# Combined FFN weights summed by accumulating DMAs, three units begun early, and six k-tiles held back, in a two-layer decoder trunk

## The chip, the cores and the metric

One core of a Trainium2 chip runs the whole program. The time is device microseconds of one execution. Three timed runs of the kernel before gave 1096.71, 1097.17 and 1097.77 us, median 1097.17.

Engines: PE multiplies matrices (the stationary operand is loaded by PEld, which overlaps), DVE is the vector engine, ACT the scalar engine, POOL the third elementwise engine, and SP only issues DMAs. SBUF is the on-chip memory, PSUM holds the accumulators of PE in eight banks of 128x512 f32.

## The reference

Input x is 512 tokens by 1024 features, f32. There are two layers, each a mixer and then a SwiGLU feed-forward network (FFN), each between two RMS norms:

```python
for i in range(DEPTH):                       # 2 layers
    h = rms_norm(x, norm_g[i, 0])
    if i % 2 == 0:
        ...                                  # differential attention + gated short convolution
        mix = jnp.concatenate([a_out, b_out], axis=-1) @ w_out_even[j]
    else:
        mix = spatial_gating(h, w_in_odd[j], ...)        # ends with @ w_out_odd[j]
    x = x + rms_norm(mix, norm_g[i, 1])
    h = rms_norm(x, norm_g[i, 2])
    f = (jax.nn.silu(h @ w_gate[i]) * (h @ w_up[i])) @ w_down[i]
    x = x + rms_norm(f, norm_g[i, 3])
```

w_gate and w_up are 1024 x 2816, w_down is 2816 x 1024, all f32.

## The kernel before

**Precision.** Each f32 operand is split into a rounded high part and a low remainder: `split` casts hi on ACT (L136) and subtracts lo on DVE (L137). A product is then three matmuls per k-tile, hi·hi, hi·lo and lo·hi.

**Blocks.** The tokens lie in four row blocks t = 0 to 3 of 128. A token-major projection (`out_proj`, its matmuls in `mm`, L110, 512 columns each) fills two PSUM banks per block. For each block `post_norm` squares the sums on ACT (L417), makes the scale on DVE and POOL (L419, L301, L307 to L310), multiplies (L453) and adds to x (L458). `pre_norm` does the same for the next norm and writes h (L431). PE then turns h (transposes, L441), and the result is split again for the next product.

**The seven products.** The FFN's first product, gate and up together, is done by a seven-product scheme instead of eight (Strassen, in Winograd's form). It cuts the k range into two halves, the tokens into first (blocks 0 and 1) and last (blocks 2 and 3), and 256 FFN columns into two, so that a unit of 256 columns is seven products of 24 matmuls of 256 columns each (`product`, L550). There are 11 units per layer. Four of the seven products use sums or differences of weight blocks, and `Unit.sum` makes them on DVE (L215, tiles `wsum`), 4 per unit, 88 in all. `Combined.fill` makes the sums on the token side when a block is turned (L388), and splits them (L382, L383).

**Weights.** `load` issues the f32 weights on SP into three tiles of 1 MB (`rawp`, names raw), in the written order of pieces. `take` and `ahead` make splits ahead of their use.

**The change of phase.** The mixer's `out_proj` holds back its last 4 k-tiles: all others go over the four blocks first, and then the held ones finish block 0, 1, 2 and 3 one after the other. So the norms and transposes of a block run beside PE's work on the next. Blocks 0 and 1 suffice for two of the seven products (7 and 3), and `EARLY = 2` units start with these while blocks 2 and 3 are still normed. The other five products of these units follow when all blocks are turned, and units 2 to 10 run their seven in a row ("steady" below).

**Order.** The program is written piece by piece. `Clock` counts PE's time (`clock.beat`), and runs the code of norms and fills when so many ns have gone by on PE (`WAITS`). The framework's scheduler then may move instructions of an engine, except where `manual_schedule` keeps the written order. Each engine executes its list strictly in order.

Of the kernel before, what the change touches and what calls it, by code (L numbers as in the profile page):

```python
# [71 lines left out]
def trunk(  # L72
# [9 lines left out]
    rawp = pool("rawp", 3)  # L82
    ap_ = pool("ap", 35)
# [21 lines left out]
    EARLY = 2  # L105
# [11 lines left out]
    class Chunk:  # L117


        def __init__(self, shape, views):  # L120
            self.shape, self.views, self.tile, self.left = shape, views, None, 0
            chunks.append(self)

        def read(self):
            self.left -= 1
            return self.tile
# [13 lines left out]
    def plan(key, chunk, part):  # L140
        chunk.left += 1
        order.append((key, [chunk], lambda: split(chunk.read()[part])))

    ALL = slice(None)

    def plan_columns(*starts, n=256):

        made = [Chunk([P, KT, n], [(ALL, col_chunk(w, c0, n))]) for w, c0 in starts]
        for j in range(n // P):
            for c in made:  # L150
                plan(None, c, (ALL, ALL, slice(j * P, (j + 1) * P)))

    def plan_wide(w, c0):

        for r in range(2):
            c = Chunk([P, 4, 512], [(ALL, col_chunk(w, c0, 512)[:, 4 * r:4 * r + 4, :])])
            for m in range(2):
                plan(None, c, (ALL, slice(2 * m, 2 * m + 2), ALL))

    def plan_rows(w, ks):  # L160

        for k in ks[::2]:
            c = Chunk([P, 2, D], [(ALL, w[k * P:(k + 2) * P, :].rearrange("(k p) f -> p k f", p=P))])
            for m in range(2):
                plan(None, c, (ALL, slice(m, m + 1), ALL))

    class Unit:
# [4 lines left out]
        READS = {1: "a", 2: "b", 4: "b", "s1": "ab", "s2": "a", "s3": "a", "s4": "b"}  # L172
        NEEDS = {5: ["s1"], 6: ["s2"], 7: ["s3"], 3: ["s4"], "s2": ["s1"], "s4": ["s2"]}
        SOON = {2: ["s1"], 4: ["s3", "s2"], 6: ["s4"]}

        def __init__(self, layer, c0):
            ws = [col_chunk(w[layer], c0, 256) for w in (w_gate, w_up)]
            self.half = {}
            for name, ks in (("a", slice(0, 4)), ("b", slice(4, 8))):
                self.half[name] = Chunk([P, 2, 4, 256], [((ALL, m), v[:, ks, :])  # L180
                                                         for m, v in enumerate(ws)])
            for names in self.READS.values():
                for n in names:
                    self.half[n].left += 1
            self.sums = {}

        def plan(self, p):
            need = [self.half[n] for n in self.reads(p)]
            order.append(((self, p), need, lambda: self.piece(p)))

        def reads(self, p):
            got = set(self.READS.get(p, ""))
            for s in self.NEEDS.get(p, []) + self.SOON.get(p, []):
                got |= self.reads(s)
            return got

        def quarter(self, name, f):
            return self.half[name].read()[:, :, :, f * P:(f + 1) * P]

        def sum(self, s):  # L200
            if s in self.sums:
                return self.sums[s]
            for before in self.NEEDS.get(s, []):
                self.sum(before)
            t = ap_.tile([P, 2, 4, P], F32, tag="a", name=nm("wsum"))
            if s == "s1":
                x, y, op = self.quarter("a", 1), self.quarter("b", 1), ALU.add
            elif s == "s2":
                x, y, op = self.sums["s1"], self.quarter("a", 0), ALU.subtract
            elif s == "s3":  # L210
                x = self.half["a"].tile[:, :, :, 0:P]
                y, op = self.quarter("a", 1), ALU.subtract
            else:
                x, y, op = self.quarter("b", 0), self.sums["s2"], ALU.subtract
            nc.vector.tensor_tensor(out=t, in0=x, in1=y, op=op)  # L215
            self.sums[s] = t
            return t

        def piece(self, p):
            if p in (1, 2, 4):  # L220
                src = self.quarter(*{1: ("a", 0), 2: ("b", 0), 4: ("b", 1)}[p])
            else:
                src = self.sum(self.NEEDS[p][0])
            made = split(src)
            for s in self.SOON.get(p, []):
                self.sum(s)
            return made

    FIRST, THEN, STEADY = (7, 3), (1, 2, 4, 6, 5), (1, 2, 4, 6, 5, 7, 3)

    def plan_ffn(layer):
        units = [Unit(layer, c * 256) for c in range(FFN // 256)]
        early, done = units[:EARLY], []
        for i, u in enumerate(early):
            for p in FIRST + ((1,) if i + 1 < EARLY else ()):
                u.plan(p)
        for i, u in enumerate(early):
            for p in THEN[1 if i + 1 < EARLY else 0:]:
                u.plan(p)
        for u in units[EARLY:]:  # L240
            for p in STEADY:
                u.plan(p)
        plan_rows(w_down[layer], range(NF))
        return units
# [19 lines left out]
    def load(upto=1000):  # L264

        while n_loaded[0] < min(upto, len(chunks)):
            if sum(c.left > 0 for c in chunks[:n_loaded[0]]) >= 3:
                return
            c = chunks[n_loaded[0]]
            c.tile = rawp.tile(c.shape, F32, tag="raw", name=nm("raw"),  # L270
                               padded_shape=[P, 2048 // math.prod(c.shape[2:])] + c.shape[2:])
            for part, view in c.views:
                if n_loaded[0] >= 2:
                    nc.sync.dma_start(out=c.tile[part], in_=view)
                else:
                    for ks in (slice(0, 2), slice(2, 4)):
                        nc.sync.dma_start(out=c.tile[:, ks, :], in_=view[:, ks, :])
            n_loaded[0] += 1

    def ahead(n):  # L280

        while len(ready) < n and n_split[0] < len(order):
            key, need, make = order[n_split[0]]
            load()
            assert all(c.tile is not None for c in need)
            ready.append((key, make()))
            n_split[0] += 1
            load()
# [74 lines left out]
    class Combined:  # L363
# [3 lines left out]

# [17 lines left out]
        def fill(self, t, banks):  # L385
# [3 lines left out]
                                                              op=ALU.subtract)  # L389
            if t < 2:  # L390
                kept = act([P, 2, 512])
                e1, e2 = (quad(kept[:, i, :]) for i in range(2))
                nc.scalar.copy(out=e1, in_=b1)
                nc.scalar.copy(out=e2, in_=b2)
                self.kept[t] = (e1, e2)
                d = quad(tmp())
                minus(d, b2, e1)
                self.put(7, t, d)
                self.put(3, t, b2)
# [142 lines left out]
    def product(bank, p, piece, hT, first, by_k):  # L542
# [5 lines left out]
        for m in range(2):  # L548
            for i, (k, a, b) in enumerate(steps):
                nc.tensor.matmul(bank[:, m * 256:(m + 1) * 256], piece[a][:, m, k, :],  # L550
# [4 lines left out]
    FIRST_TOKENS, LAST_TOKENS = slice(0, 256), slice(256, 512)  # L555

    def ffn(layer, units, hT, g_post, then, next_ahead, store=False):
# [12 lines left out]
        def finish(c, f, cols, pair_):  # L570

            nc.scalar.activation(out=c[:, 0:256], in_=c[:, 0:256], func=AF.Silu)  # L572
            nc.vector.tensor_tensor(out=pair_[:, f, cols], in0=c[:, 0:256], in1=c[:, 256:512],
                                    op=ALU.mult)
# [4 lines left out]
        early = []  # L579
        for u in units[:EARLY]:  # L580
            r, z = psum(), psum()
            run(r, u, 7)
            p7 = copied(r)
            run(z, u, 3)
            early.append((r, z, p7))
        clock.until(lambda: hT.n_turned == NT)
        for i, u in enumerate(units):
            pair_ = act([P, 2, 512])
            hidden.append(pair_)
            x, y = psum(), psum()  # L590
            run(x, u, 1)
            a = copied(x)
            run(y, u, 2)
            finish(plus(y, a), 0, LAST_TOKENS, pair_)
            if i < EARLY:
                r, z, p7 = early[i]
                run(r, u, 4, False)
                run(x, u, 6, False)
                u2 = copied(x)
# [393 lines left out]
```

## Time and profile before

| | us |
|---|---|
| median of three runs | 1097.17 |
| profiled execution | 1097.55 |
| its span on the core | 1095.8 |
| PE busy | 1065.2 (97%) |
| DVE busy | 728.5 (66%) |
| ACT busy | 496.8 (45%) |
| POOL busy | 45.2 (4%) |

The busy time of PE counts matmuls that run one into the other, and their ends are modelled. The span leaves 1.75 us of the execution's own time outside it. The mean granted clock of PE is 0.984 of full speed.

### The profile page before, as it was taken

Reading aid. Unit: us, or ns where it says so; the run is one execution under the profiler, and the core shown is the slowest. Engines: PE = TensorE matmul, PEld = TensorE weight load, DVE = VectorE, ACT = ScalarE, POOL = GpSimd, SP = SyncE. Lnnn points to the kernel's source line nnn. Section 1 sums busy time; section 2 is a strip of 40 time slices with the busy share of each in tenths; the row PEclk is TensorE's granted clock in tenths of the full one; section 3 lists DMA queues with packets and bytes.
Section 4 is the critical chain, followed back from the end, with each engine's and each line's share of the span. In section 5 each row is a group of like instructions: output and inputs, shape, how many; then the busy total and the mean of one; then the engine's idle time right before and its main releaser. Section 6 shows DMA issues by size and latency. Waiting matters only on the chain.

```text
span 1095.8 us, 15882 instructions
## 1 busy us (share of the span) xinstructions
PE 1065.2 (97%) x6527; PEld 952.4 (87%) x6527; DVE 728.5 (66%) x1083; ACT 496.8 (45%) x831; POOL 45.2 (4%) x67
## 2 busy tenths in 40 slices
PE   8999999988999999999999999988999999999997
PEld 6777778878999999988888888878999999988886
DVE  4566665598887887873328454779888787883304
ACT  4466444256544454553315333345554454573201
POOL 0011210010000000000001000010000000000000
PEclk8999999998999999999999999998999999999999
DMA  8321222313333233254202231411333323362002
GB/s 314 105 72 59 94 77 79 114 39 118 114 115 116 78 117 116 99 214 149 85 31 78 77 124 69 154 38 59 116 116 108 124 78 115 115 224 87 1 1 77
DMA packets 77770, 111.33 MB, mean 102 GB/s; under 512 B 2769, under 2 KB 63326, under 8 KB 77698
## 3 DMA queue, kind: packets, MB, share of 16 engines
q1 hardware_dynamic: 77698, 110.33, 30.2%
q8 instruction: 51, 0.84, 0.3%
q14 instruction: 21, 0.17, 0.1%
HBM read 108.21 MB, written 2.11 MB: 101 GB/s over the span
## 4 chain that ended last, share of the span: by engine, by line
PE 86%; DVE 8%; ACT 2%; issue 1%; POOL 1%; DMA 1%; SPq 0%; POOLq 0%; DVEq 0%; ACTq 0%
PE ps L110 44%; PE ps L550 38%; DVE wlo L137 1%; DVE hTlo L383 1%; POOL s L301 1%; DVE h L431 1%; ACT j L417 1%; DVE x L458 1%; PE ps L441 1%; PE ps L751 1%; DVE t L388 1%; DMA raw<-in_w_in_even_dram 1%; PE ps L937 1%; DVE wsum L215 1%; ACT whi L136 1%
## 5 line engine op out<-in xcount | busy, mean ns | idle before, releaser
L550 PE MATMUL ps<-hThi,whi 128*128 128x256 f32 x1232 | 276.3, 287 | 7.8 <-ACT hThi L382 7.3
L550 PE MATMUL ps<-hThi,wlo 128*128 128x256 f32 x1232 | 276.7, 285 | 0.0
L550 PE MATMUL ps<-hTlo,whi 128*128 128x256 f32 x1232 | 274.3, 285 | 0.0
L137 DVE TENSOR_TENSOR wlo<-raw,whi 128x1024 fp32r<-128x1024 f32 x166 | 199.0, 1223 | 65.2 <-ACT whi L136 34.4
L550 PEld LDWEIGHTS ps<-hThi,whi 128*128 128x128 f32 x1232 | 205.6, 195 | 10.1 <-ACT hThi L382 8.6
L550 PEld LDWEIGHTS ps<-hThi,wlo 128*128 128x128 f32 x1232 | 206.4, 194 | 0.1
L550 PEld LDWEIGHTS ps<-hTlo,whi 128*128 128x128 f32 x1232 | 204.9, 194 | 0.4 <-DVE hTlo L383 0.4
L136 ACT CAST whi<-raw 128x1024 fp32r<-128x1024 f32 x166 | 169.2, 1047 | 55.0 <-PE ps L110 37.4
L110 PE MATMUL ps<-whi,wlo 128*128 128x512 f32 x352 | 137.1, 390 | 0.0
L110 PE MATMUL ps<-wlo,whi 128*128 128x512 f32 x352 | 137.0, 389 | 0.0
L110 PE MATMUL ps<-whi,whi 128*128 128x512 f32 x352 | 136.7, 389 | 0.0
L137 DVE TENSOR_TENSOR wlo<-wsum,whi 128x1024 fp32r<-128x1024 f32 x88 | 105.8, 1221 | 29.5 <-ACT whi L136 25.7
L136 ACT CAST whi<-wsum 128x1024 fp32r<-128x1024 f32 x88 | 90.1, 1043 | 71.1 <-DVE wsum L215 53.6
L110 PE MATMUL ps<-whi,a 128*128 128x512 f32 x256 | 80.0, 391 | 0.0
L110 PEld LDWEIGHTS ps<-whi,whi 128*128 128x128 f32 x352 | 66.1, 188 | 13.7
L110 PEld LDWEIGHTS ps<-wlo,whi 128*128 128x128 f32 x352 | 66.1, 188 | 13.6
L110 PEld LDWEIGHTS ps<-whi,wlo 128*128 128x128 f32 x352 | 66.1, 188 | 13.5
L572 ACT ACTIVATE t<-t 128x256 f32<-128x256 f32 x88 | 36.1, 417 | 86.0 <-DVE t L562 85.8
L562 DVE TENSOR_TENSOR t<-ps,t 128x512 f32<-128x512 f32 x88 | 58.5, 686 | 15.1 <-PE ps L550 14.4
L567 ACT COPY t<-ps 128x512 f32<-128x512 f32 x70 | 40.8, 583 | 61.2 <-PE ps L550 61.0
L301 POOL TENSOR_TENSOR s<-s,neg_half 128x1 f32<-128x1 f32 (+1 forms) x40 | 25.4, 634 | 960.3 <-DVE s L419 887.2
L453 DVE TENSOR_TENSOR h<-ps,g 128x512 f32<-128x512 f32 x32 | 21.7, 685 | 63.0 <-ACT j L417 63.0
(131 smaller groups left out, 1325.4 us busy)
## 6 DMA issues: line engine op xcount, KB each, us to landing
raw<-in_w_gate_dram SPq DMA_DIRECT2D x44, 512.0 KB, 3.8
raw<-in_w_up_dram SPq DMA_DIRECT2D x44, 512.0 KB, 4.7
raw<-in_w_down_dram SPq DMA_DIRECT2D x22, 1024.0 KB, 4.8
raw<-in_w_in_even_dram SPq DMA_DIRECT2D x10, 1024.0 KB, 5.5
raw<-in_w_in_odd_dram SPq DMA_DIRECT2D x8, 1024.0 KB, 5.1
g<-in_norm_g_dram SPq DMA_DIRECT2D x8, 512.0 KB, 3.7
raw<-in_w_out_even_dram SPq DMA_DIRECT2D x4, 1024.0 KB, 4.8
raw<-in_w_out_odd_dram SPq DMA_DIRECT2D x4, 1024.0 KB, 5.0
```

What stands on the lines that cost most here:

```text
L110: nc.tensor.matmul(out, lhsT, rhs, start=start, stop=stop)
L136: nc.scalar.copy(out=hi, in_=src)
L137: nc.vector.tensor_tensor(out=lo, in0=src, in1=hi.bitcast(F32), op=ALU.subtract)
L215: nc.vector.tensor_tensor(out=t, in0=x, in1=y, op=op)
L301: nc.gpsimd.tensor_tensor(out=y0[:, :n], in0=a, in1=neg_half[:, :n], op=ALU.pow)
L383: nc.vector.tensor_tensor(out=lo, in0=src, in1=hi.bitcast(F32), op=ALU.subtract)
L388: minus = lambda out, x, y: nc.vector.tensor_tensor(out=out, in0=x, in1=y, op=ALU.subtract)
L453: nc.vector.tensor_tensor(out=f[:, c], in0=halves[n], in1=g[:, c], op=ALU.mult)
L550: nc.tensor.matmul(bank[:, m * 256:(m + 1) * 256], piece[a][:, m, k, :], hT.at(b, p)[:, k, :], start=first and m == 0 and i == 0, stop=i = ...
L562: nc.vector.tensor_tensor(out=c, in0=x, in1=y, op=ALU.add)
L567: nc.scalar.copy(out=c, in_=x)
L572: nc.scalar.activation(out=c[:, 0:256], in_=c[:, 0:256], func=AF.Silu)
```

## The change

- `Chunk` becomes a 512-KB piece of four k-tiles by 256 columns, which lives in the common pool of 41 tiles (before: 35, and three of 1 MB). When a piece has been split, a DMA issued by POOL (L128 of the changed kernel) adds the next weight block to it in place; then it is split again. A unit has one piece that goes through products 4, 5, 6 and 3 (three accumulations), one through 1 and 7 (one), and one for 2. That is four accumulations per unit, 88 in all, 512 KB each. The DVE sums (L215) are gone. Up to 6 pieces may be on their way.
- The scheme's form changes, so that products 1 and 2 need the first tokens only. `EARLY = 3` units begin with these two. `SLOTS` mixes the products of neighbouring units: the four uses of a piece stand three products apart.
- gate and up are now the two column halves of a bank. A unit has two silus of 128x512 instead of four of 128x256, and two closing multiplications instead of four.
- `fill` makes five combinations of blocks 2 and 3, and none of blocks 0 and 1.
- The mixer's `out_proj` holds 6 k-tiles instead of 4, and the norms' waits are other numbers.
- From there until all four blocks are turned (`settled`), PE, ACT and DVE keep the written order.

The diff, cut to its core (the lines that are renamed alone or follow from it are left out):

```diff
-    rawp = pool("rawp", 3)
-    ap_ = pool("ap", 35)
+    ap_ = pool("ap", 41)
...
-    EARLY = 2
+    EARLY = 3
...
         def read(self):
             self.left -= 1
-            return self.tile
+            made = split(self.tile)
+            if self.more:
+                nc.gpsimd.dma_start(out=self.tile, in_=self.more.pop(0), accum_op=ALU.add)
+            return made
...
         def piece(self, p):
-            if p in (1, 2, 4):
-                src = self.quarter(*{1: ("a", 0), 2: ("b", 0), 4: ("b", 1)}[p])
-            else:
-                src = self.sum(self.NEEDS[p][0])
...
+            if p not in self.chunk:
+                v = self.views
+                if p == 1:
+                    self.chunk[1] = self.chunk[7] = Chunk(v[0, 0], v[1, 0])
+                elif p == 2:
+                    self.chunk[2] = Chunk(v[0, 1])
+                elif p == 4:
+                    self.chunk.update(dict.fromkeys(
+                        (4, 5, 6, 3), Chunk(v[1, 1], v[1, 0], v[0, 0], v[0, 1])))
+            plan((self, p), self.chunk[p])
...
-    FIRST, THEN, STEADY = (7, 3), (1, 2, 4, 6, 5), (1, 2, 4, 6, 5, 7, 3)
+    SLOTS = {4: 0, 5: 3, 2: 4, 1: 5, 6: 6, 7: 8, 3: 9}
+    EARLY_SLOTS = {4: 0, 5: 3, 6: 6, 7: 7, 3: 9}
...
-            if sum(c.left > 0 for c in chunks[:n_loaded[0]]) >= 3:
+            if sum(c.left > 0 for c in chunks[:n_loaded[0]]) >= 6:
...
             else:
                 e1, e2 = self.kept[t - 2]
-                self.put(1, t, b1)
-                t1, t2, t4 = (quad(tmp()) for _ in range(3))
+                t1, t2, t3, t4, l2 = (quad(tmp()) for _ in range(5))
                 minus(t1, e1, b1)
-                minus(t2, e2, t1)
-                self.put(2, t, b2)
-                minus(t4, b2, t2)
+                self.put(5, t, t1)
+                less(t2, t1, b2)
+                self.put(6, t, t2)
+                less(t4, t2, e2)
                 self.put(4, t, t4)
-                self.put(6, t, t2)
-                self.put(5, t, t1)
+                self.put(3, t, b2)
+                nc.scalar.copy(out=l2, in_=b2)
+                minus(t3, l2, b1)
+                self.put(7, t, t3)
...
+            if n == 2 * EARLY:
+                clock.until(lambda: hT.n_turned == NT)
+                settled()
...
-    out_proj(Mixed([mixed[k] for k in MIX_ORDER]), 4, g_post,
-             lambda t: pre_norm(t, g_pre, hT, WAITS), (1, 2, 3))
+    settled = in_order()
+    out_proj(Mixed([mixed[k] for k in MIX_ORDER]), 6, g_post,
+             lambda t: pre_norm(t, g_pre, hT, (4500, 2200)), (1, 2, 3), wait=3300)
```

Two places show how the order of instructions moves. The first is DVE's list in layer 0, up to the h of block 3. Before (tiles h_2186 and x_84 are block 3's; hTlo and t without a weight's name belong to the fill of block 2, s to the norms):

```order
L388 TENSOR_TENSOR t_2300<-a_2080,ps_2286 128x512
L310 SCALAR_TENSOR_TENSOR s_2230<-s_2229,s_2194 128x1
L383 TENSOR_TENSOR hTlo_2306<-ps_2291,hThi_2305 128x4x128
L458 SCALAR_TENSOR_TENSOR x_84<-h_2186,s_2230,x_84 128x512 x2
L388 TENSOR_TENSOR t_2301<-a_2080,t_2300 128x512
L388 TENSOR_TENSOR t_2302<-ps_2291,t_2301 128x512
L419 SCALAR_TENSOR_TENSOR s_2237<-s_2236,eps_t 128x1
L307 TENSOR_TENSOR s_2277<-s_2243 128x1
L308 SCALAR_TENSOR_TENSOR s_2278<-s_2277,s_2237 128x1
L310 SCALAR_TENSOR_TENSOR s_2279<-s_2278,s_2243 128x1
L383 TENSOR_TENSOR hTlo_2311<-t_2302,hThi_2310 128x4x128
L431 SCALAR_TENSOR_TENSOR h_2283<-x_84,s_2279,g_1772 128x512 x2
```

After, the same end (x_81 is block 3; the fill of block 2 ends just above, wlo_2298 and wlo_2350 are the low parts of weights for unit 1's product 2 and unit 2's product 1, t_2344 is unit 0's sum of products 1 and 2):

```order
L140 TENSOR_TENSOR wlo_2298<-raw_1887,whi_2297 128x1024
L266 TENSOR_TENSOR s_2308<-s_2215 128x1
L267 SCALAR_TENSOR_TENSOR s_2309<-s_2308,s_2209 128x1
L269 SCALAR_TENSOR_TENSOR s_2310<-s_2309,s_2215 128x1
L417 SCALAR_TENSOR_TENSOR x_81<-h_2207,s_2310,x_81 128x512 x2
L378 SCALAR_TENSOR_TENSOR s_2317<-s_2316,eps_t 128x1
L519 TENSOR_TENSOR t_2344<-ps_2296,t_2294 128x512
L140 TENSOR_TENSOR wlo_2350<-raw_1893,whi_2349 128x1024
L266 TENSOR_TENSOR s_2375<-s_2323 128x1
L267 SCALAR_TENSOR_TENSOR s_2376<-s_2375,s_2317 128x1
L269 SCALAR_TENSOR_TENSOR s_2377<-s_2376,s_2323 128x1
L390 SCALAR_TENSOR_TENSOR h_2381<-x_81,s_2377,g_1799 128x512 x2
```

The whole fill of block 2, two weight splits and a unit's sum now stand ahead of block 3's h. Before, the fill of block 2 lay between the steps of the norm, part of it behind the h, and no weight split stood there.

The second is ACT's list in a steady unit of layer 0. Before (whi from wsum or raw are casts, the copies empty a PSUM bank, ACTIVATE is silu):

```order
L567 COPY t_3750<-ps_3715 128x512
L572 ACTIVATE t_3710<-t_3710 128x256
L572 ACTIVATE t_3780<-t_3780 128x256
L136 CAST whi_3786<-wsum_3679 128x1024
L136 CAST whi_3814<-wsum_3721 128x1024
L136 CAST whi_3844<-raw_3486 128x1024
L136 CAST whi_3872<-raw_3683 128x1024
L567 COPY t_3842<-ps_3715 128x512
L136 CAST whi_3912<-raw_3683 128x1024
L136 CAST whi_3954<-wsum_3918 128x1024
L567 COPY t_3902<-ps_3715 128x512
```

After, around the copy t_3816 of product 1 (raw_3367, raw_3201 and raw_3430 are pieces that are cast, added to by DMA, and cast again):

```order
L524 COPY t_3685<-ps_3556 128x512
L139 CAST whi_3692<-raw_3367 128x1024
L139 CAST whi_3726<-raw_3201 128x1024
L139 CAST whi_3756<-raw_3430 128x1024
L528 ACTIVATE t_3721<-t_3721 128x512
L139 CAST whi_3786<-raw_3367 128x1024
L139 CAST whi_3821<-raw_3201 128x1024
L139 CAST whi_3855<-raw_3430 128x1024
L524 COPY t_3816<-ps_3785 128x512
```

The second casts of three pieces now follow their first casts with one silu between, and the copy of product 1 stands behind the last of them. On POOL the three accumulations between these casts stand next to each other.

## Rows read from the trace of the kernel before

**Rows 1.** The page: span, busy time by engine, the engines' shares of the last chain.
```profile
span 1095.8 us, 15882 instructions
...
PE 1065.2 (97%) x6527; PEld 952.4 (87%) x6527; DVE 728.5 (66%) x1083; ACT 496.8 (45%) x831; POOL 45.2 (4%) x67
...
PE 86%; DVE 8%; ACT 2%; issue 1%; POOL 1%; DMA 1%; SPq 0%; POOLq 0%; DVEq 0%; ACTq 0%
```

**Rows 2.** The chain that ended last, in order of time: start us, us, what.
```profile
175.65 37.22 PE ps L110 x164
...
284.33 181.01 PE ps L550 x1506
```

**Rows 3.** Busy time by window: length, busy (x count) by engine, PE clock, DMA share, GB/s.
```profile
230.81:268.88 38.07, 30.23 (x211) 28.67 (x210) 34.36 (x58) 22.07 (x39) 2.47 (x3) 0.87 0.25 84
731.88:770.47 38.59, 30.50 (x213) 29.36 (x212) 34.56 (x59) 21.59 (x39) 2.48 (x3) 0.87 0.22 69
...
308.40:328.60 20.20, 20.20 (x171) 20.20 (x170) 16.46 (x19) 9.73 (x14) 0.00 (x0) 1.00 0.37 120
```

**Rows 4.** Timeline of PE: start us, us, what, [idle before <- releaser].
```profile
230.58 0.39 PE L110 MATMUL ps<-wlo,a 128*128 128x512 f32 x1
234.67 0.58 PE L550 MATMUL ps<-hThi,whi 128*128 128x256 f32 x1 [3.71 <-ACT hThi L382]
...
237.52 0.41 PE L550 MATMUL ps<-hThi,whi 128*128 128x256 f32 x1
237.74 0.41 PE L550 MATMUL ps<-hThi,wlo 128*128 128x256 f32 x1
...
242.80 1.23 PE L441 MATMUL ps<-ident,h 128*128 128x128 f32 x8 [0.43 <-DVE h L431]
...
253.30 1.97 PE L441 MATMUL ps<-ident,h 128*128 128x128 f32 x8 [3.52 <-DVE h L431]
```

**Rows 5.** Timeline of DVE, same stretch.
```profile
241.90 1.41 DVE L431 SCALAR_TENSOR_TENSOR h<-x,s,g 128x512 f32<-128x512 f32 x2
...
247.84 1.41 DVE L458 SCALAR_TENSOR_TENSOR x<-h,s,x 128x512 f32<-128x512 f32 x2
...
250.50 0.21 DVE L419 SCALAR_TENSOR_TENSOR s<-s,eps_t 128x1 f32<-128x1 f32 x1
251.43 0.16 DVE L307 TENSOR_TENSOR s<-s 128x1 f32<-128x1 f32 x1 [0.72 <-POOL s L301]
...
252.49 1.41 DVE L431 SCALAR_TENSOR_TENSOR h<-x,s,g 128x512 f32<-128x512 f32 x2
```

**Rows 6.** By line and shape: busy us, mean ns of one | idle before <- releasers.
```profile
L137 DVE TENSOR_TENSOR wlo<-wsum,whi 128x1024 fp32r<-128x1024 f32 x88 | 105.8, 1221 | 29.5 <-ACT whi L136 25.7 <-PE ps L550 3.9
L136 ACT CAST whi<-wsum 128x1024 fp32r<-128x1024 f32 x88 | 90.1, 1043 | 71.1 <-DVE wsum L215 53.6 <-PE ps L550 17.2
...
L562 DVE TENSOR_TENSOR t<-ps,t 128x512 f32<-128x512 f32 x88 | 58.5, 686 | 15.1 <-PE ps L550 14.4 <-ACT t L567 0.7
...
L567 ACT COPY t<-ps 128x512 f32<-128x512 f32 x70 | 40.8, 583 | 61.2 <-PE ps L550 61.0
...
L215 DVE TENSOR_TENSOR wsum<-raw,raw 128x1024 f32<-128x1024 f32 x22 | 26.8, 1218 | 0.4 <-DMA raw<-in_w_up_dram 0.4
...
L382 ACT CAST hThi<-t 128x512 fp32r<-128x512 f32 x16 | 9.5, 618 | 3.5 <-DVE t L388 3.5
...
L383 DVE TENSOR_TENSOR hTlo<-ps,hThi 128x512 fp32r<-128x512 f32 x12 | 8.2, 685 | 0.0
...
L572 ACT ACT_TABLE_LOAD x2 | 2.6, 1283 | 6.2 <-DVE t L562 6.2
```

**Rows 7.** DMA issues: count, KB each, median us from issue to landing.
```profile
raw<-in_w_gate_dram SPq DMA_DIRECT2D x44, 512.0 KB, 3.8
raw<-in_w_up_dram SPq DMA_DIRECT2D x44, 512.0 KB, 4.7
...
x<-in_x_dram SPq DMA_DIRECT2D x3, 512.0 KB, 11.1
```

More of the change, by code (lines that the diff above doesn't have):

```diff
@@ L187, in plan @@
[L187 to L212, printed above, removed]
-            else:
[L214 to L217, printed above, removed]
@@ new lines, in trunk, with unit_steps @@
+    SLOTS = {4: 0, 5: 3, 2: 4, 1: 5, 6: 6, 7: 8, 3: 9}
+    EARLY_SLOTS = {4: 0, 5: 3, 6: 6, 7: 7, 3: 9}
+    def unit_steps(units):
+        steps = []
+        for i, u in enumerate(units):
+            at = 5 * min(i, EARLY) + 7 * max(i - EARLY, 0)
+            slots = EARLY_SLOTS if i < EARLY else SLOTS
+            steps += [(at + n, u, p) for p, n in slots.items()]
+        steps.sort(key=lambda step: step[0])
+        return [(u, p) for u in units[:EARLY] for p in (1, 2)] + [step[1:] for step in steps]
@@ L231, in plan_ffn @@
     def plan_ffn(layer):
         units = [Unit(layer, c * 256) for c in range(FFN // 256)]
[L233 to L242, printed above, removed]
+        steps = unit_steps(units)
@@ L243, in plan_ffn @@
+        for u, p in [steps[0], steps[1], (units[0], 4)] + steps[2:2 * EARLY]:
+            u.piece(p)
+        for u, p in steps[2 * EARLY:]:
+            if (u, p) != (units[0], 4):
+                u.piece(p)
         plan_rows(w_down[layer], range(NF))
@@ L282, in ahead @@
         while len(ready) < n and n_split[0] < len(order):
-            key, need, make = order[n_split[0]]
+            key, chunk = order[n_split[0]]
             load()
-            assert all(c.tile is not None for c in need)
-            ready.append((key, make()))
+            assert chunk.tile is not None
+            ready.append((key, chunk.read()))
             n_split[0] += 1
@@ L553, in product, with ffn @@
                 clock.beat(115.0)
-    FIRST_TOKENS, LAST_TOKENS = slice(0, 256), slice(256, 512)
-    def ffn(layer, units, hT, g_post, then, next_ahead, store=False):
+    def ffn(layer, units, hT, g_post, then, next_ahead, settled, store=False):
         hidden = []
@@ L568, in copied, with gate, close @@
             return c
[L570 to L574, printed above, removed]
+        def gate(c):
+            nc.scalar.activation(out=c, in_=c, func=AF.Silu)
+            return c
+        def close(u, half, g, c):
+            nc.vector.scalar_tensor_tensor(
+                out=u.hidden[:, :, 256 * half:256 * half + 256],
+                in0=c.rearrange("p (m t) -> p m t", m=2), scalar=-1.0,
+                in1=g.rearrange("p (m t) -> p m t", m=2), op0=ALU.mult, op1=ALU.mult)
@@ new lines, in ffn @@
+        for u in units:
+            u.hidden = None
+        for n, (u, p) in enumerate(unit_steps(units)):
+            if n == 2 * EARLY:
+                clock.until(lambda: hT.n_turned == NT)
+                settled()
+            if u.hidden is None:
+                u.hidden = act([P, 2, 512])
+                hidden.append(u.hidden)
+            if p == 1:
+                u.x = psum()
+                run(u.x, u, 1)
+                u.a = copied(u.x)
+                if hasattr(u, "y"):
+                    u.g = gate(plus(u.y, u.a))
+            elif p == 2:
+                u.y = psum()
+                run(u.y, u, 2)
+                if hasattr(u, "a"):
+                    u.g = gate(plus(u.y, u.a))
+            elif p == 4:
+                u.w = psum()
+                run(u.w, u, 4)
+            elif p == 5:
+                u.q = psum()
+                run(u.q, u, 5)
+            elif p == 6:
+                run(u.x, u, 6, False)
+                u.u2 = copied(u.x)
+            elif p == 7:
+                run(u.x, u, 7, False)
+                u.u3 = copied(u.x)
+                close(u, 0, u.g, plus(u.w, u.u3))
+                u.up = plus(u.q, u.u3)
+            else:
+                run(u.q, u, 3, False)
+                close(u, 1, gate(plus(u.q, u.u2)), u.up)
@@ L624, in trunk @@
     for t in range(1, NT):
-        load(t)
+        load(2 * t)
         nc.sync.dma_start(out=xs[t], in_=x[0, t * P:(t + 1) * P, :])
```

127 lines of the change are left out of this document (35 added, 92 removed).

## The prediction

> **What bounds the kernel now.** I read the page first, then the chain of waits, then the windows around the places where the chain leaves PE, and only there the timelines. The page says that PE is busy for 97% of the span and that 86% of the last chain is PE; DVE has 8% of it [rows 1]. The chain shows where: the steady part of an FFN is one piece of 1506 matmuls of 256 columns in 181.01 us, 0.1202 us each, with no wait of another engine in it [rows 2]. One unit there takes 168 x 0.1202 = 20.2 us, and in 20.2 us DVE is busy for 16.46 and ACT for 9.73 [rows 3]. So the 4 sums of 1.22 us [rows 6] that the change takes from DVE in each unit come off an engine that is not waited for: **worth 0 in steady units.** Work removed gains nothing there; a wait that is added costs its full length.
>
> What can be gained lies at the change of phase, from the mixer's out_proj to the FFN. In layer 0 the window from 230.81 to 268.88 is 38.07 us long [rows 3]. It holds 192 products of 256 columns (23.1 us), 16 transposes and 3 longer matmuls (1.7 together): 24.8 us of work, so 13.3 us are lost, and 13.8 in layer 1's window of 38.59. The timeline names the idle pieces: 3.71 us for the cast of a combination on ACT, 0.43 and 3.52 us for block 2's and block 3's h on DVE [rows 4]. What remains is mostly PE at half speed: behind an idle stretch the products stand 0.22 us apart (237.52, 237.74) [rows 4] instead of 0.12, until 238.1, which costs some 1.5 us each time. The whole of both changes of phase, 27 us, is the most that the change can win.
>
> **The change part by part.** I work from the profiled execution, 1097.55 us; the median of the three runs is 0.4 lower.
>
> *Change of phase.* More matmuls now lie beside blocks 0 to 2: a block has 6 held k-tiles, 36 matmuls of 512 columns at 37.22/164 = 0.227 us [rows 2], so 8.2 us instead of 5.4. I expect no idle before block 2's h: 4.1 us of idle gone. But from there to block 3's h the written order counts, and it is DVE's list that decides. Before, those two h end at 243.31 and 253.90, 10.6 us apart [rows 5]. In the new order DVE does between them: 9 steps of the fill at 0.69 (6.2), 3 low parts at 1.22 (3.7), two halves of the multiplication at 0.69 (1.4), x and h at 1.41 each (2.8), a unit's sum 0.69, and 8 small steps of 0.16 to 0.21 (1.4): 16.2 us [rows 5, 6]; instructions that follow without a wait overlap by some 0.08 us, so 14.3. To it come its waits. Four low parts of the fill need a cast on ACT just before, 0.62 each, and one step needs a copy, 0.58: 3.1. The cast whi_2297 stands behind a copy on ACT: 0.8. The squares of x: the add ends at 249.25 and the scale begins at 250.50, 1.25 [rows 5]; POOL's 0.72 is covered by a low part. And wlo_2350 needs whi_2349, which stands on ACT behind the first silu, whose table load takes 1.28 us [rows 6]: 1.28 + 0.62 + 1.04 = 2.9. Sum 14.3 + 3.1 + 0.8 + 1.25 + 2.9 = 22.4 us. PE has 71 products (8.5) and 8 transposes (1.0) for that time: 12.9 us idle, against 3.52 before. So up to block 3's transposes it is 12.9 - 7.7 = 5.2 us worse per layer.
>
> Behind them PE has 55 products (6.6 us) that need no new tokens, while block 3's fill runs; they cover it up to product 4. Product 5 of unit 0 needs the second cast of its piece, and that stands in ACT's and DVE's lists behind the fill's rest and a silu: about 0.69 + 0.58 + 0.69 + 0.62 + 0.69 + 0.69 + 0.62 + 1.04 + 1.22 = 6.8 us against the 2.9 of product 4. I count 2.3 of these 3.9, since steps overlap. In sum +7.5 per layer, **+15 in all**. Bounds: if all the waits hide, 14.3 us stand against 9.5, 4.8 idle, less than the 7.7 before, and with the late product 5 the sum is 0; with nothing overlapped it is +11 per layer. So 0 to +22.
>
> *Accumulations.* The trace of before has no DMA that POOL issues. In a steady unit the new lists tie them into a ring. The copy of product 1 stands on ACT behind three second casts, the last of which waits for the third accumulation; product 6 needs that copy, since it writes to the same bank. From product 6's start to product 7's end PE has 63 products: 7.6 us. Then ACT copies (0.58), DVE does 3 low parts and 3 sums and one closing step (3.7 + 2.1 + 0.7 = 6.5, each cast beside it), POOL issues the third accumulation, A us pass, ACT casts (1.04) and copies product 1 (0.58). The ring is 16.3 + A us [rows 2, 6]. A unit's matmuls take 20.2. So **A may be 3.9 us**; each us more costs 1 us in each of some 14 such units (7 per layer).
>
> The rows nearest to A: a load of the same 512 KB takes 3.8 us, the second of a pair issued together 4.7, and a load in the crowded start 11.1 [rows 7]. Standing behind one other costs 0.9. The third accumulation stands behind two, 3.8 + 1.8 = 5.6; as they come some us apart, I take 5.2. That is 1.3 over, x 14 = **+18**. Bounds: 3.8 gives 0, 11.1 gives +101.
>
> For POOL's DMAs the Trainium skill (DMA: Bandwidth & Descriptors, section "Anatomy of one DMA — SWDGE (gpsimd) path") states about 2.0 us and bytes/436e3 more; the estimate for 512 KB is 3.2 us. By it the accumulations would hide and the sum would be without this term. No run yet shows such a DMA.
>
> *Ends of layers.* The last unit has no other unit's products between its own 1, 6 and 7, which share a bank: copy and hand-over, 0.58 and some 0.25, are bare twice, and product 3 may wait for its last piece. 0 to 4 us per layer; I take 1.5, **+3**.
>
> *The rest.* In the mixers' projections pieces of 512 KB replace 1 MB; PE is the chain there as well, and the first load is 512 KB either way: 0, within 1 either way. Two silus instead of four, fewer closings: off the path.
>
> **Sum: 1097.5 + 15 + 18 + 3 = 1133.5 us**, say 1133.
>
> **The rivals.**
> - *Accumulations hidden* (A up to 3.9). For it: the row of 3.8 us and a DMA share of 0.37 in a steady unit [rows 3, 7]. Against it: three issued close together. Time 1097.5 + 15 + 3 = 1115.
> - *Accumulations heavy.* If adding in place moves each byte twice, one takes 3.8 + 0.9 = 4.7 and the third behind two 4.7 + 2 x 1.8 = 8.3: 4.4 x 14 = 62, time 1177. Nothing in the trace shows for or against it but the 0.9. The Trainium skill (same page, section "Rules for kernel authors") says that the accumulate reads its destination and writes it later, which speaks for twice the bytes; no run here shows it yet.
> - *Faster: the change of phase clears.* If DVE gets from block 2's h to block 3's within 9.5 us (its 14.3 us of work not all in the way, because some of it waits for nothing and PE's list leaves room), and A is below 3.9, the three units' early products cover all: up to 27 us less, 1071; half of it, 1084, is what I would expect. For it: 48 more matmuls that need the first tokens only. Against: DVE's list is fixed there and longer by its own count.
> - *Nothing to see*: the ends meet, 1097.
>
> **How the numbers follow.** My forecast 0.37 (own range 1120 to 1152), hidden 0.27 (1104 to 1120), heavy 0.19 (1152 to 1200), faster 0.13, no change 0.04. A change within 0.2%, 2.2 us, could not be told from none. Faster 0.13, same 0.04, slower 0.83. The range leaves out most of the faster case and the upper part of the heavy one: 1097 to 1185.
>
> **What would show it.** Right: idle of PE between block 2's and block 3's transposes of 10 us or more, released by DVE h or ACT casts; then in each steady unit a gap of 1 to 2 us at product 6, released by the copy of product 1 on ACT, which itself waited for an accumulation; accumulations of over 5 us from issue to landing. Hidden: those gaps are absent and only the two changes of phase are longer. Wrong altogether: the window from the mixer's last held product to block 3's transposes is shorter than before, or PE waits at places where I count nothing, such as casts that wait for plain loads.

## The result and the profile after

The changed kernel takes 1304.43 us (median of four runs, 1301.07 to 1307.79), against 1097.47 before (the three runs of above and a fourth): ratio 1.1887, 95% interval 1.1855 to 1.1918. It is slower by 207 us. I had forecast slower, 1133 us and at most 1185; the direction was right and the size wrong.

The page after, its parts 1, 3, 4 and 6 (in part 3: queue, packets, MB, share of 16 engines' span; in part 6: us from issue to landing):

```profile
span 1299.4 us, 16125 instructions
...
PE 1113.3 (86%) x6527; PEld 994.0 (77%) x6527; DVE 627.1 (48%) x951; ACT 495.5 (38%) x787; POOL 158.0 (12%) x155
...
q1 hardware_dynamic: 81186, 98.79, 24.5%
q0 software_dynamic: 46464, 46.14, 23.7%
...
PE 56%; DMA 20%; DVE 9%; issue 7%; ACT 6%; POOL 1%; SPq 0%; POOLq 0%; DVEq 0%; ACTq 0%
...
raw<-in_w_gate_dram SPq DMA_DIRECT2D x44, 512.0 KB, 4.8
raw<-in_w_up_dram POOLq DMA_DIRECT2D x44, 512.0 KB, 8.1
raw<-in_w_gate_dram POOLq DMA_DIRECT2D x44, 512.0 KB, 7.0
```

In [rows 1] PE had 86% of the last chain and DMA 1%; now PE has 56% and DMA 20%. The new queue q0 holds the 88 accumulations. By the time that its packets took they have 23.7% of 1299.4 us, 308 us of all 16 engines, for 46.14 MB: 150 GB/s, where the plain loads of q1 get 98.79 MB through in 318 us, 310 GB/s. The mean packet has some 1.0 KB on q0 and 1.2 KB on q1, so the packets' length hardly explains the difference (more on it at e8_wide_runs). From issue to landing an accumulation takes 7 to 8 us in the median, against the 3.8 and 4.7 of [rows 7]. DVE's busy time fell from 728.5 to 627.1 us (the sums are 88 x 1.22 = 107), and this is worth nothing: e4_dve_sums below, which has the sums on DVE, has no gap in its steady units.

One steady unit, by busy time in windows (the columns of [rows 3]):

```profile
core 0: us, PE busy (x) PEld busy (x) DVE busy (x) ACT busy (x) POOL busy (x), PEclk, DMA share, GB/s
...
398.50:429.40 30.90, 23.00 (x169) 22.76 (x169) 12.06 (x14) 9.93 (x13) 5.18 (x4) 0.83 0.63 119
```

It takes 30.9 us, where [rows 3] show 20.2 for the same matmuls. Who closes the ring is seen in the chain that ended last, in the same window (start us, us, what):

```profile
398.55 15.44 PE ps L509 x105
...
414.62 1.16 DVE wlo L140
...
416.48 11.24 DMA raw<-in_w_up_dram
...
427.80 1.04 ACT whi L139
428.84 0.49 ACT t L524
...
429.38 2.72 PE ps L509 x11
```

PE works 105 products to 414, a low part ends at 415.8, POOL issues the accumulation at 416.48, it lands 11.24 us later, ACT casts at 427.80 and copies product 1 at 428.84, and only then can product 6 write to that bank, at 429.38. PE's timeline has the gap and its releaser (idle before, in brackets):

```profile
398.55 0.58 PE L509 MATMUL ps<-hThi,whi 128*128 128x256 f32 x1 [7.03 <-ACT t L524]
...
429.38 0.58 PE L509 MATMUL ps<-hThi,whi 128*128 128x256 f32 x1 [7.85 <-ACT t L524]
```

On POOL and ACT (timelines) the clump of three is seen:

```profile
413.16 1.28 POOL L128 DMA_DIRECT2D raw<-in_w_up_dram  x1 [12.21 <-DVE wlo L140]
414.06 1.71 POOL L128 DMA_DIRECT2D raw<-in_w_gate_dram  x1
416.48 1.29 POOL L128 DMA_DIRECT2D raw<-in_w_up_dram  x1 [0.70 <-issue]
```

```profile
419.21 1.05 ACT L139 CAST whi<-raw 128x1024 fp32r<-128x1024 f32 x1 [3.84 <-DMA raw<-in_w_up_dram]
423.94 1.04 ACT L139 CAST whi<-raw 128x1024 fp32r<-128x1024 f32 x1 [3.69 <-DMA raw<-in_w_gate_dram]
427.80 1.04 ACT L139 CAST whi<-raw 128x1024 fp32r<-128x1024 f32 x1 [2.81 <-DMA raw<-in_w_up_dram]
428.75 0.58 ACT L524 COPY t<-ps 128x512 f32<-128x512 f32 x1
```

Issued at 413.2, 414.1 and 416.5, they land at 419.2, 423.9 and 427.8: 4.7 and 3.9 us one behind the other. In the 14 steady units the accumulation on the chain lands 10.4 to 13.5 us after its issue, 11.9 in the mean. PE's idle time, added up over its timeline, is 179.1 us, where before it is 23.7, and PE's busy time grew from 1065.2 to 1113.3: 155 + 48 us, the whole difference of the spans. The 48 us fit with products at half speed behind the gaps, the effect that [rows 4] show behind 3.7 us: the mean granted clock is 0.916 of full speed, where before it is 0.984.

The change of phase in layer 0, PE's timeline:

```profile
232.32 1.03 PE L400 MATMUL ps<-ident,h 128*128 128x128 f32 x8
...
244.57 0.58 PE L509 MATMUL ps<-hThi,whi 128*128 128x256 f32 x1 [4.75 <-ACT whi L139]
...
254.95 1.97 PE L400 MATMUL ps<-ident,h 128*128 128x128 f32 x8 [5.33 <-DVE h L390]
```

Block 2's and block 3's transposes lie 22.6 us apart; in [rows 4] it was 10.5.

### The profile page after: what moved, and what is told of

Same layout as the page of the kernel before. It is cut to its first block, busy times and chain, and to the rows that moved or that the text cites. A ratio compares the mean times of both kernels' runs of the same rounds, so it can differ in the third digit from the quotient of the medians.

```text
span 1299.4 us, 16125 instructions
## 1 busy us (share of the span) xinstructions
PE 1113.3 (86%) x6527; PEld 994.0 (77%) x6527; DVE 627.1 (48%) x951; ACT 495.5 (38%) x787; POOL 158.0 (12%) x155
## 3 DMA queue, kind: packets, MB, share of 16 engines
q1 hardware_dynamic: 81186, 98.79, 24.5%
q0 software_dynamic: 46464, 46.14, 23.7%
## 4 chain that ended last, share of the span: by engine, by line
PE 56%; DMA 20%; DVE 9%; issue 7%; ACT 6%; POOL 1%; SPq 0%; POOLq 0%; DVEq 0%; ACTq 0%
PE ps L109 36%; PE ps L509 17%; DMA raw<-in_w_up_dram 12%; DMA raw<-in_w_gate_dram 7%; DVE wlo L140 3%; ACT whi L139 3%; DVE hTlo L341 1%; ACT j L376 1%; ACT t L524 1%; ACT hThi L340 1%; DVE h L412 1%; DVE h L390 1%; PE ps L712 1%; POOL s L260 1%; PE ps L907 1%
## 5 line engine op out<-in xcount | busy, mean ns | idle before, releaser
L140 DVE TENSOR_TENSOR wlo<-raw,whi 128x1024 fp32r<-128x1024 f32 x254 | 306.0, 1223 | 271.8 <-ACT whi L139 249.3
L509 PE MATMUL ps<-hThi,whi 128*128 128x256 f32 x1232 | 300.2, 307 | 156.6 <-ACT t L524 138.2
L139 ACT CAST whi<-raw 128x1024 fp32r<-128x1024 f32 x254 | 258.9, 1047 | 263.9 <-DMA raw<-in_w_up_dram 126.8
L509 PEld LDWEIGHTS ps<-hThi,whi 128*128 128x128 f32 x1232 | 223.5, 211 | 164.3 <-ACT t L524 142.6
L509 PE MATMUL ps<-hThi,wlo 128*128 128x256 f32 x1232 | 295.8, 301 | 4.0 <-DVE wlo L140 3.9
L509 PEld LDWEIGHTS ps<-hThi,wlo 128*128 128x128 f32 x1232 | 224.4, 211 | 5.8 <-DVE wlo L140 5.8
L128 POOL DMA_DIRECT2D raw<-in_w_gate_dram x44 | 61.1, 1388 | 256.7 <-DVE wlo L140 256.7
L128 POOL DMA_DIRECT2D raw<-in_w_up_dram x44 | 57.1, 1298 | 231.3 <-DVE wlo L140 194.4
L376 ACT ACTIVATE j<-ps 128x512 bf16<-128x512 f32 x32 | 19.1, 597 | 117.8 <-PE ps L109 117.6
L109 PE MATMUL ps<-hThi,whi 128*128 128x512 f32 x224 | 61.0, 403 | 0.0
```

The costliest lines, as they stand in the source:

```text
L109: nc.tensor.matmul(out, lhsT, rhs, start=start, stop=stop)
L128: nc.gpsimd.dma_start(out=self.tile, in_=self.more.pop(0), accum_op=ALU.add)
L139: nc.scalar.copy(out=hi, in_=src)
L140: nc.vector.tensor_tensor(out=lo, in0=src, in1=hi.bitcast(F32), op=ALU.subtract)
L376: nc.scalar.activation(out=junk(512), in_=parts[n], func=AF.Square, scale=1.0 / 32.0, accum_out=ms[:, n:n + 1])
```

## The experiments

All times are medians; each ratio is to the kernel before on the same chip (1097.8 to 1097.9 us). The diffs show the core of each edit against the changed kernel; `...` stands for lines left out, and long lines are broken. My theory after the result: adding in place costs the DMA engines twice the time of a plain load, three such transfers in a clump stand in a ring of ACT, DVE, POOL and PE, and the rest (some 30 us) is the written order in the change of phase.

**e1_pool_plain: the same DMAs without the addition.**

```diff
-                nc.gpsimd.dma_start(out=self.tile, in_=self.more.pop(0), accum_op=ALU.add)
+                nc.gpsimd.dma_start(out=self.tile, in_=self.more.pop(0))
```

> The changed kernel, with each of the 88 DMAs on POOL's queue as a plain load over the piece instead of an accumulation (the sums are left out); every engine's list is the same. Theory (adding in place keeps the 16 DMA engines twice as long, 3.5 us instead of 1.7 for 512 KB, so the third of a clump lands after 11 us): the third lands after 6 to 7 us, a steady unit takes 22 to 23.5 us instead of 31, and the time is 1140 to 1170 us. Rival 1 (POOL's software queue itself is slow, whatever it moves): landing and time stay, 1290 to 1305. Rival 2 (the new order of PE, ACT and DVE is at fault): 1280 or more.

Measured: 1162.91 us, ratio 1.0592 (1.0571 to 1.0614). Queue and landing:

```profile
q0 software_dynamic: 12672, 46.14, 12.2%
...
raw<-in_w_up_dram POOLq DMA_DIRECT2D x44, 512.0 KB, 4.4
raw<-in_w_gate_dram POOLq DMA_DIRECT2D x44, 512.0 KB, 4.5
```

The same bytes on the same queue now take 12.2% of 1159.4 us, 141 us: 326 GB/s, more than twice the 150 of the accumulations, and land after 4.4. So it is the addition and not POOL's queue that is slow; 1304.4 - 1162.9 = 141.5 of the 207 us go with it. The gaps at product 6 are 1.1 to 3.2 us. The third load of a clump, in the chain of one unit:

```profile
407.39 6.27 DMA raw<-in_w_up_dram
```

In the 14 steady units the load on the chain takes 4.4 to 6.7 us, 5.6 in the mean, near the 5.2 that the prediction took for an accumulation. POOL issues the third 3.1 us behind the first, in the unit of above 3.3, so it is not the issuing that grew.

**e2_sp_plain: the same loads issued by SP.**

```diff
-                nc.gpsimd.dma_start(out=self.tile, in_=self.more.pop(0), accum_op=ALU.add)
+                nc.sync.dma_start(out=self.tile, in_=self.more.pop(0))
```

> As e1_pool_plain, with these 88 plain loads issued by SP (the sums are left out). Theory: a load lands after 4 to 5 us, the ring of a steady unit closes within its 20.2 us of matmuls, and what stays is the change of phase: 1105 to 1125 us. Rival 1 (POOL's queue): the same here. Rival 2 (the order): 1200 or more. If SP's strict order holds up other loads behind these: 1130 to 1160, with SP waiting for DVE's low parts.

Measured: 1133.09 us, ratio 1.0323 (1.0299 to 1.0347), 8 us above what the theory allowed. It lies in the range given to SP's strict order, but this run doesn't show that to be the reason. Against e1_pool_plain 29.8 us are gone, so who issues the loads counts too, if far less than the addition; the loads on the chain in its steady units take 3.8 to 5.6 us. Gaps of 0.4 to 1.8 us at product 6 are left. Most of the rest is the change of phase and the layers' ends, which I had put at 18.

**e3_half_bytes: accumulations of half the size.**

```diff
+                nc.gpsimd.dma_start(out=self.tile[:, 0:2, :],
+                                    in_=self.more.pop(0)[:, 0:2, :], accum_op=ALU.add)
```

> The changed kernel with accumulations of two of the four k-tiles only, 256 KB each (the other half of the sums is left out); the count of DMAs on POOL is the same. Theory (cost by bytes, twice a plain load's): the third lands after 6 to 8 us, 1135 to 1175 us. Rival 1 (a fixed cost of each of POOL's DMAs): landing hardly shorter, 1270 or more. Rival 2 (the order): 1280 or more.

Measured: 1226.6 us, ratio 1.1172 (1.1143 to 1.1202): outside all that was expected. The queue:

```profile
q0 software_dynamic: 23936, 23.07, 13.3%
...
raw<-in_w_up_dram POOLq DMA_DIRECT2D x44, 256.0 KB, 5.3
raw<-in_w_gate_dram POOLq DMA_DIRECT2D x44, 256.0 KB, 4.8
```

The engines' time halves (13.3% of 1222.2 us, 163 us, instead of 308), so that part does go by bytes. But the landing falls only from 8.1 and 7.0 to 5.3 and 4.8: if a landing is a fixed time and one by size, twice the one minus the other leaves some 2.5 us that do not depend on the size (an estimate). I had left that part out.

**e8_wide_runs: the same bytes in runs of 2 KB.**

```diff
+            wide = [col_chunk(w[layer], min(c0, FFN - 512), 512) for w in (w_gate, w_up)]
+            self.wide = {(f, k): v[:, 4 * k:4 * k + 2, :]
+                         for f, v in enumerate(wide) for k in range(2)}
...
+                nc.gpsimd.dma_start(out=self.tile.rearrange("p a b -> p (a b)")
+                                    .rearrange("p (k f) -> p k f", k=2),
+                                    in_=self.more.pop(0), accum_op=ALU.add)
```

> The changed kernel with each accumulation of 512 KB reading rows of 512 columns of two k-tiles, 2 KB in a run, instead of 256 columns of four, 1 KB in a run (other weights are added, so the sums are not those of the scheme). Theory (cost by bytes, each moved twice): 1290 to 1310 us. Rival (cost by run or packet): the busy share of POOL's queue falls towards half, 1210 to 1240 us.

Measured: 1288.99 us, ratio 1.1744 (1.172 to 1.1767), one us below the theory's range.

```profile
q0 software_dynamic: 23936, 46.14, 22.0%
```

The packets halve (23936 instead of 46464), the engines' time falls only from 308 to 283 us. The cost is by bytes, with a small part by packet: worked out from these two runs (an estimate), accumulations in the 12672 packets of e1_pool_plain would still take some 270 us, against the 141 of the plain loads.

**e5_unread_sums: the traffic without the wait, not tied to its place.**

```diff
+                nc.gpsimd.dma_start(out=dummy[n_dummy[0] % 2], in_=self.more.pop(0), accum_op=ALU.add)
+                n_dummy[0] += 1
```

> The changed kernel with its 88 accumulations of 512 KB going into two tiles that nothing reads; the casts read the plainly loaded pieces again (the sums are left out; the common pool has 39 tiles instead of 41 to make room). Theory (the accumulations cost as a wait in the ring, not as traffic): the gaps at product 6 vanish although the DMA engines are as busy, 1120 to 1150 us. Rival (they fill the DMA engines and hold up the plain loads and everything behind): 1200 us or more, with casts that wait for SP's loads.

Measured: 1300.31 us, ratio 1.1847 (1.1823 to 1.187). This doesn't tell the two apart. Nothing tied the accumulations to their place, so the scheduler put them all at the front, where POOL's list also has the attention's steps:

```profile
DVE t L701 <- POOL t L698: 111.1, 15, 35.5
...
POOL dummy L132 <- DMA dummy<-in_w_up_dram: 99.5, 40, 9.1
POOL dummy L132 <- DMA dummy<-in_w_gate_dram: 96.8, 40, 7.1
```

POOL waited 196 us for its own DMAs, and DVE 111 us for POOL. In the FFN, where no accumulation was left, PE ran 1290 products in 157.5 us without a gap (its chain: 487.38 to 644.89).

**e9_unread_paced: the same, each accumulation tied to its place.**

```diff
+                d = dummy[n_dummy[0] % 4]
+                nc.vector.tensor_copy(out=d[:, 0, 0:1], in_=made[1].bitcast(F32)[:, 0, 0:1])
+                nc.gpsimd.dma_start(out=d, in_=self.more.pop(0), accum_op=ALU.add)
```

> As e5_unread_sums, but each accumulation into an unread tile is tied, by a copy of one column on DVE, to the low part after which the changed kernel issues it; four such tiles, 37 tiles in the common pool, sums left out. So the traffic comes when it comes in the changed kernel. Theory (the wait costs): no gaps of 7 to 10 us at product 6, 1120 to 1160 us. Rival (the traffic costs: plain loads stand behind the accumulations): 1200 us or more, with casts that wait for SP's loads.

Measured: 1126.49 us, ratio 1.0264 (1.0245 to 1.0283), as the theory had it. Queue, and a stretch of steady units:

```profile
q0 software_dynamic: 46464, 46.14, 26.4%
...
dummy<-in_w_up_dram POOLq DMA_DIRECT2D x44, 512.0 KB, 7.9
dummy<-in_w_gate_dram POOLq DMA_DIRECT2D x44, 512.0 KB, 9.4
```

```profile
core 0: us, PE busy (x) PEld busy (x) DVE busy (x) ACT busy (x) POOL busy (x), PEclk, DMA share, GB/s
340.00:360.00 20.00, 20.00 (x166) 19.79 (x166) 11.83 (x17) 8.91 (x11) 4.97 (x4) 1.00 0.95 184
```

All 46 MB are accumulated beside the units, each landing after 8 to 9 us in the median, with a DMA share of 0.95, and PE has no gap. So the traffic costs nothing and the wait costs 1304.4 - 1126.5 = **178 us**. It is rather 180: this kernel first clears four tiles on POOL, and the attention's transposes come at 100.01 us instead of 97.55. The share adds up the time of packets and passes 1 (1.16 from 800 to 820 us), so 0.95 does not say that the engines are nearly full.

**e7_ahead5: a longer lead.**

```diff
-        def run(bank, u, p, first=True, more=3):
+        def run(bank, u, p, first=True, more=5):
```

> The changed kernel with weights split five pieces ahead instead of three; accumulations as they are, nothing left out. Theory (a latency in a ring): with a longer lead the gap of 8 us at product 6 shrinks to 0 to 4 us, 1160 to 1230 us; the DMA engines' own time, 4 x 3.5 + 3 x 1.7 = 19 us of a unit's 20.2, leaves little room. Rival (no slack in the DMA engines, the unit is bound by them): 1270 or more.

Measured: 1217.94 us, ratio 1.1096 (1.1066 to 1.1127), in the theory's range. The gaps at product 6 are up to 5.2 us, but block 3's transposes now wait 15.3 us for its h, since more splits stand ahead of it.

**e11_one_by_dma: one accumulation per unit, three sums on DVE** (from e6_dve_free below).

```diff
+            self.by_dma = len(self.more) == 1
...
+            if self.by_dma and self.more:
+                nc.gpsimd.dma_start(out=self.tile, in_=self.more.pop(0), accum_op=ALU.add)
+            elif hasattr(self, 'extra') and self.left:
```

> As e6_dve_free, nothing left out, with one of the four sums of each unit (product 1's piece to product 7's) made by an accumulating DMA on POOL again and three on DVE. Theory (a lone accumulation lands in 5 to 6 us and has that much slack): 1099 to 1106 us, like e6_dve_free. Rival (every accumulation in the ring costs its length): 1115 us or more.

Measured: 1193.09 us, ratio 1.0878 (1.0853 to 1.0904): my figure for a lone accumulation was wrong too, and the rival holds. POOL's and ACT's timelines:

```profile
407.91 1.30 POOL L134 DMA_DIRECT2D raw<-in_w_up_dram  x1 [26.18 <-DVE wlo L149]
```

```profile
415.89 1.99 ACT L148 CAST whi<-raw 128x1024 fp32r<-128x1024 f32 x2 [5.54 <-DMA raw<-in_w_up_dram]
...
420.31 0.58 ACT L534 COPY t<-ps 128x512 f32<-128x512 f32 x1
```

Issued at 407.91, the only accumulation of the unit lets ACT go on at 415.89, 8 us later; the copy of product 1 stands behind three casts on ACT, at 420.31, one of which waits for a sum on DVE besides. A quarter of the traffic, with the wait, costs 91 us over e6_dve_free; all of it without the wait cost none. It also bears out the prediction's ring: with 3.9 us of slack, 8 us should cost 4.1 in a unit, and the units lie 25.4 us apart in layer 0 and 26.7 in layer 1, 5.2 and 6.5 more than 20.2. The rest is slower products behind the gaps and the wait for the sum.

**e4_dve_sums: the new order, with the sums on DVE.**

```diff
+                nc.sync.dma_start(out=self.extra, in_=self.more.pop(0))
...
-                nc.gpsimd.dma_start(out=self.tile, in_=self.more.pop(0), accum_op=ALU.add)
...
+                nc.vector.tensor_tensor(out=self.tile, in0=self.tile, in1=self.extra, op=ALU.add)
+                self.fetch()
```

`fetch` lets SP load the next block into a tile of its own.

> The changed kernel with the weight blocks loaded by SP into tiles of their own and added on DVE, 88 additions of 128x1024; nothing is left out. Theory: the accumulations' cost is gone and DVE has 4 x 1.22 us more in each unit, which fits (about 17 of 20.2 us): 1105 to 1130 us. Rival 2 (the order): 1200 or more. A third way: DVE's longer list in the change of phase makes block 3's h later still: up to 1150.

Measured: 1128.55 us, ratio 1.0276 (1.0259 to 1.0293). The steady units have no gaps left (1535 products in 186.99 us); PE is idle 1.15 + 6.54 + 0.68 + 6.58 us around blocks 2 and 3.

**e6_dve_free: that kernel without the written order.**

```diff
-        held.enter_context(tc.manual_schedule(engines={E.PE, E.Activation, E.DVE}))
```

> As e4_dve_sums (sums on DVE, nothing left out, 1128.6 us), without the written order of PE, ACT and DVE in the change of phase. Theory A (the fill, two low parts and a silu standing ahead of block 3's h by the written order make the idle 6.5 + 6.6 us): 1105 to 1118 us. Theory B (the amount of DVE work makes it, wherever it stands): 1124 to 1134 us.

Measured: 1102.18 us, ratio 1.0038 (1.0023 to 1.0052). In the kernel with the sums on DVE the written order costs 26.4 us, more than theory A gave it. What remains, in PE's timeline of layer 0, is one gap at the change of phase and three at the layer's end:

```profile
458.87 0.39 PE L516 MATMUL ps<-hThi,whi 128*128 128x256 f32 x1 [0.67 <-ACT t L531]
...
462.74 0.39 PE L516 MATMUL ps<-hThi,whi 128*128 128x256 f32 x1 [0.73 <-ACT t L531]
...
467.86 0.58 PE L516 MATMUL ps<-hThi,whi 128*128 128x256 f32 x1 [2.00 <-DVE t L526]
```

**e10_ends_table: that, with the ends of layers mended and silu's table loaded early.**

```diff
+    LAST_SLOTS = {4: 0, 1: 0.5, 5: 1.3, 6: 1.6, 2: 1.8, 7: 1.9, 3: 4}
...
+            slots = EARLY_SLOTS if i < EARLY else LAST_SLOTS if u is units[-1] else SLOTS
...
+        nc.scalar.activation(out=warm, in_=warm, func=AF.Silu)
```

The lines come on top of e6_dve_free; the last stands ahead of the mixer's out_proj.

> As e6_dve_free (1102.2 us, against 1097.9 of before), nothing left out, with two more edits: the last unit of a layer mixes its products with those of the unit before it so that its copies are covered, and a silu of one column ahead of the mixer's out_proj brings the table load forward. Theory: the three gaps of 0.7 + 0.7 + 2.0 us at the end of each layer go (6.8 us in all), and 1 to 2 us in layer 0's change of phase: 1093 to 1096 us, faster than before by 2 to 5. Rival (gaps move to the start of the FFN's second product): 1098 to 1103 us.

Measured: 1092.25 us, ratio 0.9950 (0.9937 to 0.9962): faster than both kernels, by 5.5 us against before, and 0.8 us better than forecast. The three gaps are gone, and one of 0.64 us per layer at the second product has come; the gap at the change of phase is 5.2 us instead of 6.15.

## Why the prediction was wrong

**What bounds the kernel**: right. DVE lost 101 us of work and nothing came of it.

**Change of phase, from h to h: right.** The sum was 22.4 us between block 2's and block 3's h; DVE's timeline after:

```profile
230.70 1.41 DVE L390 SCALAR_TENSOR_TENSOR h<-x,s,g 128x512 f32<-128x512 f32 x2
...
235.85 0.69 DVE L341 TENSOR_TENSOR hTlo<-t,hThi 128x512 fp32r<-128x512 f32 x1 [0.69 <-ACT hThi L340]
...
244.55 1.23 DVE L140 TENSOR_TENSOR wlo<-raw,whi 128x1024 fp32r<-128x1024 f32 x1 [0.74 <-ACT whi L139]
...
248.63 0.22 DVE L378 SCALAR_TENSOR_TENSOR s<-s,eps_t 128x1 f32<-128x1 f32 x1 [0.94 <-ACT j L376]
...
252.43 1.23 DVE L140 TENSOR_TENSOR wlo<-raw,whi 128x1024 fp32r<-128x1024 f32 x1 [2.97 <-ACT whi L139]
...
254.14 1.41 DVE L390 SCALAR_TENSOR_TENSOR h<-x,s,g 128x512 f32<-128x512 f32 x2
```

The h end at 232.11 and 255.55, 23.4 us apart. The waits came one by one as reckoned: 0.69 for each of the fill's casts (0.62 in the sum), 0.74 for whi_2297 (0.8), 0.94 for the squares (1.25), 2.97 for the cast behind the silu and its table (2.9). PE's loss between the two sets of transposes is 22.6 - 9.5 = 13.1 us, where I had 12.9 idle; 4.75 + 0.68 + 5.33 = 10.8 are idle, the rest is slower products.

**Change of phase and ends as a whole: too small by some 9 us.** I had 15 + 3; e9_unread_paced, which has all but the waits for accumulations, is 28.7 us slower than before, and 1.8 of this comes at its start (its transposes of 100.01 us are at 98.23 before). Its idle time on PE shows which step failed. There is none before block 2's h, as forecast. Around block 3:

```profile
247.61 0.58 PE L516 MATMUL ps<-hThi,whi 128*128 128x256 f32 x1 [5.32 <-ACT whi L146]
...
258.17 1.97 PE L407 MATMUL ps<-ident,h 128*128 128x128 f32 x8 [5.52 <-DVE h L397]
```

The gaps there are 5.32 + 0.68 + 5.52 + 1.20 + 0.88 = 13.6 us in layer 0, where [rows 4] have 7.7, and 12.4 against 7.9 in layer 1: +10 in both, which the 15 covers. The ends of layers have 0.68 + 0.73 + 2.00 = 3.4 each, 6.8 in all: "I take 1.5" was too little. And PE's busy time is 1073.4 us instead of 1065.2: 8 us more, for which my sum has no term, although I had found 1.5 us of half speed behind each idle stretch of before. With the sums on DVE, 26.4 us go without the written order (e4_dve_sums to e6_dve_free), and mending the ends together with silu's table gives 9.9 (e6_dve_free to e10_ends_table). No run with accumulations was without the written order, so for the changed kernel itself this share is not shown.

**Accumulations: the ring was right, its size A was not, and this is the step that put the time outside the range.** "The third accumulation stands behind two, 3.8 + 1.8 = 5.6; as they come some us apart, I take 5.2." It measures 11.2 in the unit shown. Put into the prediction's own sum this gives (11.2 - 3.9) x 14 = 102 instead of 18 and 1218 us in all, outside the range already. The prediction had named 11.1 us as a bound, and left the time that it gives out of its range. The steady units lie 30.7 us apart instead of 20.2, which is 10.5 x 14 = 147 us; the early units, which the sum left out, have some 10 us of such gaps in each layer besides, with half speed behind them. Three things were mis-sized:
- The time of 512 KB on the engines. I took 0.9 us from the difference of two landings [rows 7]. An accumulation takes 3.5 us of all 16 engines (308 us / 88), a plain load on the same queue 1.6 (141 / 88).
- The doubling, which I gave to a rival at 0.19, is what happens to the time on the engines: 150 GB/s against 326 with the addition left out. Whether each byte moves twice, no run shows. The sentence of the Trainium skill (DMA: Bandwidth & Descriptors, section "Rules for kernel authors") that the accumulate reads its destination and writes it later agrees with this ratio. The same page's figure for a DMA of POOL (section "Anatomy of one DMA — SWDGE (gpsimd) path"), 2.0 us and bytes/436e3, an estimate of 3.2 us for 512 KB, agrees with no row here: a plain one lands after 4.4 us in the median, beside other loads, a lone accumulation after some 8. With 0.9 doubled the heavy rival itself came to 8.3 us and 1177; three times 3.5 would have given over 10.
- The ring's own length. From product 6's start to product 7's copy it is 398.55 to 408.88, 10.3 us, where I had 7.6: after a gap PE runs at half speed (the granted clock is 0.83 in the window of 398.5 to 429.4), which makes the ring longer in turn. 16.3 + 11.2 + 2.7 = 30.2, against 30.8 for this unit.

What stays open: what inside the DMA takes twice the time; which of the steps in the written order cost most of its 26.4 us (the whole order was taken away at once), and how far a lead longer than five pieces would take the accumulations, since the longer lead tried here also moved block 3's h.

## What to carry to other kernels

When work moves from an engine with slack to a DMA, price the DMA as a latency in the ring that waits for it, and price its time on the DMA engines from a queue's bytes and share of busy time, not from differences between landings. A transfer that nobody waits for was free here even at a DMA share of 0.95; one that stands in front of a copy in an engine's list costs what exceeds the slack of its ring, and in a clump of three the last waits for the two before it. Before an order is written out by hand, see what the scheduler's own order gives: here the new form of the scheme with sums on DVE and the scheduler's order, its ends mended, beats both kernels, the one before by 0.5%.

## What the runs showed of the hardware

- By the time that their packets took, accumulating DMAs from HBM into SBUF run at 150 GB/s over 16 engines (the changed kernel), plain ones on the same queue at 326 (e1_pool_plain), on SP's queue at 310 (the changed kernel). Longer runs, 2 KB instead of 1, bring 163 (e8_wide_runs).
- Plain loads on POOL's queue move in 12672 packets for 46.14 MB, 3.6 KB in the mean; as accumulations the same transfers take 46464 packets, 1.0 KB in the mean.
- POOL itself is busy for 1.3 to 1.7 us with each issue of an accumulation, and for 0.75 us with that of a plain load (e1_pool_plain).
- PE loses twice in a gap: the 155 us of added idle time came with 48 us of products at half speed.
